# A transformer block on one core: one wide k-tile of the opening in two chunks, and the second norm's factor ahead of the last transposes

## The chip, the core and the metric

The kernel runs on one core of a Trainium2 chip. The core has a matrix engine (TensorE, PE in the profile; its weight loads are listed as PEld), a vector engine (DVE), a scalar engine (ACT), GpSimd (POOL), and a queue engine (SP) that here only issues DMAs. Each engine works through its own list of instructions in order; semaphores hold an instruction until what it needs is there. The metric is the device time of one execution in microseconds (us), the median of three runs.

## The reference, cut to what matters

A residual block on 256 tokens of width 2048, all in 32-bit floats: a norm, one input projection that gives the columns of an attention and of a convolution, an output projection with a residual, a second norm, and a gated feed-forward layer of 5632 hidden columns.

```python
xn = rms_norm(h, norm1_g)
proj = einsum('bsd,dn->bsn', xn, w_in)          # 5120 columns: q, k, v and conv
att = diff_attention(q, k, v, lam); u = conv(...)
h = h + einsum('bsm,md->bsd', concat(att, u), w_out)
hn = rms_norm(h, norm2_g)                        # the second norm
a, bu = einsum(hn, w_gate), einsum(hn, w_up)
h = h + einsum('bsf,fd->bsd', silu(a) * bu, w_down)
```

## The kernel before, in words

**Split products.** Each 32-bit product is made of three matmuls: operands are split into a high part (`hi`, a cast on ACT) and a rest (`lo`, a subtraction on DVE), and PE adds hi·hi, lo·hi and hi·lo. So each weight tile passes through four steps: SP loads it (`raw`, L320), ACT casts it (`whi`, L325), DVE subtracts (`wlo`, L334), PE multiplies (L364, L365 with `whi`, then L370 with `wlo`). One such tile with its matmuls is a *chunk*: two k-tiles (rows of 128) by 512 columns, 512 KB and 12 matmuls. There are five `raw` buffers, three `whi` and three `wlo`. Both row blocks of 128 tokens (m = 0, 1) are multiplied in each chunk.

**Order.** Python writes the instructions in one pass over the list of chunks (`run_chunks`). Ahead of each chunk's matmuls stand the load, cast and subtraction of a later chunk: one chunk ahead while the number is below `OPENING`, two ahead after that. All other work is in generators (`start`, `yield`): after the first and the second half of each chunk's matmuls each running generator is taken one step further, so a `yield` puts the next step half a chunk later on every engine's list. What a step issues stands on its engine behind what was issued before, and waits there in order.

**Opening.** The first two 512-column blocks of the input projection (`("i", 0)` and `("i", 1)`) are accumulated together, so that the first k-tiles of x are used twice while x still arrives. K-tile 0 comes in two chunks of 512 columns (256 KB each, 6 matmuls each), k-tiles 1 to 3 in one chunk each of 1024 columns (512 KB, 12 matmuls, L397, L398, L402 in `multiply_wide`), the rest as everywhere. `XLOADS` says ahead of which chunk which k-tiles of x are loaded (L484); `x_split` casts and subtracts x (`xhi` on ACT, `xlo` on DVE). All these loads stand in one queue, SP's.

**Second norm.** `out_done(n)` takes 512 finished columns of the output projection, adds them to h (DVE, L822), transposes h in two steps of two 128-column tiles (PE, `ps_h`, L832), scales and splits them (ACT L837, L839, DVE L840), takes sums of squares (ACT, L478) and sends h to DRAM (issued by POOL). After the last n = 3 the sums are reduced (DVE, L851) and `rsqrt_mean` gives the factor `rstd` on POOL (L222, L223). Then `make_forms` starts: it spreads the factor over the columns (`rep` on ACT, L976; two transposes `ps_r` on PE, L980; `rb` copied by ACT, L983), multiplies the transposed h (`hn`) by it in four steps (DVE, L988), and makes hi and lo of it (`chi`, `clo`) and seven sums with their hi and lo (`sums`, `fhi`, `flo`), which the feed-forward layer needs from its second block on. The first block of the feed-forward layer, 16 chunks of `w_gate` and `w_up`, needs none of them, and runs meanwhile on the unscaled h. In the text its chunks are counted t0 to t15; t3 is the one at whose end the new order transposes the factor.

**Pairs.** The later blocks have chunks of another kind (`wb`, `wt`, `wh`, `wlt`, `wlb`; L1041 to L1070): 21 matmuls whose operands DVE and ACT prepare from sums of weights. `hn` lies in the buffers of `wb`, so the first pair's loads wait for the last reads of `hn`.

Of the kernel before, what the change touches and what calls it, by code (L numbers as in the profile page):

```python
# [12 lines left out]
F32 = mybir.dt.float32  # L13
F32R = mybir.dt.float32r
AF = mybir.ActivationFunctionType
ALU = mybir.AluOpType
AX = mybir.AxisListType

P = 128
D = 2048  # L20
S = 256
NM = S // P
# [8 lines left out]
KD = D // P  # L31
N = 512

LINE = 128
EPS = 1e-6
# [13 lines left out]
NK = 2  # L49

WARM = 17

WIDE = 4
XLOADS = {0: range(0, 1), 2: range(1, 2), 3: range(2, 4), 5: range(4, 8), 7: range(8, 12), 9: range(12, 16)}
XSQUARES = 4

XWHOLE = 40

OPENING = 2 + WIDE - 1 + (KD - WIDE) // NK

CONV_TILES = 2

# [66 lines left out]
def tile_block(  # L129
# [6 lines left out]
    act, dve, pool, pe, sp = nc.scalar, nc.vector, nc.gpsimd, nc.tensor, nc.sync  # L136
# [8 lines left out]
    small = prestack.enter_context(tc.tile_pool(name="small", bufs=4))  # L145
# [4 lines left out]
    h = [pre.tile([P, D], F32, tag=f"h{m}", name=f"h{m}", bufs=1) for m in range(NM)]  # L150
    away = ctx.enter_context(tc.tile_pool(name="away", bufs=1, space=bass.MemoryType.DRAM))
    hd = [away.tile([P, D], F32, tag=f"hd{m}", name=f"hd{m}") for m in range(NM)]
# [65 lines left out]
    def rsqrt_mean(dst, ss, n, eps):  # L218

        k = dst.shape[-1]  # L220
        t = small.tile([P, 8], F32, tag="rsq", name="rsq")
        pool.tensor_scalar(t[:, :k], ss, 1.0 / n, eps, ALU.mult, ALU.add)  # L222
        pool.tensor_tensor(dst, t[:, :k], neghalf[:, :k], ALU.pow)  # L223
# [69 lines left out]
    def block(w, cols, ks, xs, done=None, bkey=None, first=True, last=True, spare=False, cuts=()):  # L293

        ks = list(ks)
        cols = [(cols, N)] if isinstance(cols, int) else cols
        width = sum(n for _, n in cols)
        bkey = bkey if bkey is not None else ("b", len(chunks))
        i = 0
        cuts = list(cuts)  # L300
        while i < len(ks):
            part = ks[i : i + (cuts.pop(0) if cuts else NK * N // width)]
            i += len(part)
            chunks.append(dict(w=w, ks=part, k0=part[0], nk=len(part), cols=cols, width=width, xs=xs, bkey=bkey,
                               first=part[0] == ks[0] and first, last=last and i == len(ks),
                               done=done if i == len(ks) else None, spare=spare, by_dma=False,
                               rows=slice(part[0], part[-1] + 1), load=load_chunk, round=round_chunk,
                               split=split_chunk, multiply=multiply))
# [167 lines left out]
    def square_sum(src, accum, **kw):  # L476
        junk = pre.tile([P, N], F32, tag="junk", name="junk", bufs=1)
        act.activation(junk[:, : src.shape[-1]], src, AF.Square, accum_out=accum, **kw)  # L478
# [336 lines left out]
    ss2 = [const.tile([P, 4], F32, tag=f"ss2_{m}", name=f"ss2_{m}") for m in range(NM)]  # L815
    rstd2s = const.tile([P, NM], F32, tag="rstd2", name="rstd2")
    rstd2 = [rstd2s[:, m : m + 1] for m in range(NM)]

    def out_done(n, ps):
        cs = slice(n * N, (n + 1) * N)  # L820
        for m in range(NM):
            dve.tensor_tensor(h[m][:, cs], h[m][:, cs], ps[m], ALU.add)  # L822
        if n == 2:
            held[0] -= NM
        yield
        for t in range(0, N // P, 2):
            k = n * (N // P) + t
            yield from room(1)
            pt = aux_ps.tile([P, 2, S], F32, tag="aux", name="ps_h")
            for i in range(2):  # L830
                for m in range(NM):
                    pe.transpose(pt[:, i, m * P : (m + 1) * P], h[m][:, (k + i) * P : (k + i + 1) * P], ident)  # L832
            if k % HK == 0:
                hn.append(early.tile([P, HK, S], F32, tag="wb", name="hn"))
            rows = hn[k // HK][:, k % HK : k % HK + 2, :]
            for i in range(2):
                act.activation(rows[:, i, :], pt[:, i, :], AF.Copy, scale=col("g2", k + i))  # L837
            hi, lo = lhs_two("h", k)
            act.copy(hi, rows)  # L839
            dve.tensor_tensor(lo, rows, hi.bitcast(F32), ALU.subtract)  # L840
            for i in range(2):
                hT[k + i] = (hi[:, i, :], lo[:, i, :])
            yield
        for m in range(NM):
            square_sum(h[m][:, cs], ss2[m][:, n : n + 1])
            pool.dma_start(out=hd[m][:, cs], in_=h[m][:, cs])
        if n == D // N - 1:
            yield
            ss = small.tile([P, NM], F32, tag="ssh", name="ssh")
            for m in range(NM):  # L850
                dve.tensor_reduce(ss[:, m : m + 1], ss2[m], AX.X, ALU.add)  # L851
            rsqrt_mean(rstd2s, ss, D, EPS)
            yield
            yield
            prestack.close()
            ffn["pool"] = ctx.enter_context(tc.tile_pool(name="ffn", bufs=1))
            start(make_forms())
# [114 lines left out]
    def make_forms():  # L972
        fp = ffn["pool"]
        rep = fp.tile([P, S], F32, tag="sum1", name="rep")
        for m in range(NM):
            act.activation(rep[:, m * P : (m + 1) * P], ident, AF.Identity, bias=rstd2[m], scale=0.0)  # L976
        yield
        ps = aux_ps.tile([P, N], F32, tag="aux", name="ps_r")
        for m in range(NM):
            pe.transpose(ps[:, m * P : (m + 1) * P], rep[:, m * P : (m + 1) * P], ident)  # L980
        yield
        rb = fp.tile([P, S], F32, tag="sum2", name="rb")
        act.copy(rb, ps[:, :S])  # L983
        yield
        for i in range(2):
            for k in range(0, HK, 4):
                t = hn[i][:, k : k + 4, :]
                dve.tensor_tensor(t, t, rb.unsqueeze(1).to_broadcast([P, 4, S]), ALU.mult)  # L988
                yield

        nr = HK - NS
        chi = fp.tile([P, 2 * nr, S], F32R, tag="chi", name="chi")
        clo = fp.tile([P, 2 * nr, S], F32R, tag="clo", name="clo")
        for i in range(2):
            act.copy(chi[:, i * nr : (i + 1) * nr], hn[i][:, NS:])
        yield
        for i in range(2):
            dve.tensor_tensor(clo[:, i * nr : (i + 1) * nr], hn[i][:, NS:],
                              chi[:, i * nr : (i + 1) * nr].bitcast(F32), ALU.subtract)
            yield  # L1000
        forms.update(plain={k: (chi[:, i, :], clo[:, i, :]) for i, k in enumerate(REST)})
        a11, a21 = (hn[0][:, :NS, m * P : (m + 1) * P] for m in range(NM))
        a12, a22 = (hn[1][:, :NS, m * P : (m + 1) * P] for m in range(NM))
        fhi = fp.tile([P, 7, NS, P], F32R, tag="fhi", name="fhi")
        flo = fp.tile([P, 7, NS, P], F32R, tag="flo", name="flo")
        f = fp.tile([P, 7, NS, P], F32, tag="wh", name="sums", bufs=2)
        dve.scalar_tensor_tensor(f[:, 4], a21, -1.0, a22, ALU.mult, ALU.subtract)
        dve.scalar_tensor_tensor(f[:, 5], f[:, 4], -1.0, a11, ALU.mult, ALU.subtract)
        act.copy(fhi[:, 0], a11)
        act.copy(fhi[:, 1], a12)  # L1010
        act.activation(fhi[:, 3], a22, AF.Copy, scale=-1.0)
        yield
        dve.tensor_tensor(f[:, 6], a11, a21, ALU.subtract)
        dve.tensor_tensor(f[:, 2], a12, f[:, 5], ALU.subtract)
        act.copy(fhi[:, 4:7], f[:, 4:7])
        act.copy(fhi[:, 2], f[:, 2])
        yield
        for i, a in ((0, a11), (1, a12)):
            dve.tensor_tensor(flo[:, i], a, fhi[:, i].bitcast(F32), ALU.subtract)
        yield  # L1020
        dve.scalar_tensor_tensor(flo[:, 3], a22, -1.0, fhi[:, 3].bitcast(F32), ALU.mult, ALU.subtract)
        dve.tensor_tensor(flo[:, 2], f[:, 2], fhi[:, 2].bitcast(F32), ALU.subtract)
        yield
        dve.tensor_tensor(flo[:, 4:7], f[:, 4:7], fhi[:, 4:7].bitcast(F32), ALU.subtract)
        forms.update(pair={f: (fhi[:, f], flo[:, f]) for f in range(7)})
# [246 lines left out]
    fx, fh = xT.get, hT.get  # L1272
# [2 lines left out]
    for b in range(2):  # L1275
        done += [lambda ps, key=key, b=b: qk_done(key, b, ps) for key in "kq"]
    done += [lambda ps, b=b: v_done(b, ps) for b in range(2)]
    for i in range(2):
        block(w_in, i * N, range(1), fx, bkey=("i", i), last=False, spare=i == 1)
    for k in range(1, WIDE):  # L1280
        block(w_in, [(0, 2 * N)], range(k, k + 1), fx, bkey=("i",), first=False, last=False)
        chunks[-1]["multiply"] = multiply_wide
    for i, d in enumerate(done):
# [83 lines left out]
```

## Time and profile before

| | us |
|---|---|
| median of 3 runs (lowest, highest) | 1034.31 (1033.91, 1034.35) |
| the profiled execution | 1033.71 |
| its span, first to last instruction | 1031.9 |
| PE busy | 1026.1 |
| DVE busy | 928.7 |
| ACT busy | 643.2 |
| POOL busy | 103.0 |

The span lies 1.8 us below the profiled execution's own time; this is what lies around the instructions. The execution is 0.60 us below the median of the runs. Timelines below have as columns: start and length in us, engine, line, operation, tiles written and read, shapes, count, and in brackets the idle time ahead and what ended it. A matmul's length is that of its whole passage, and matmuls overlap: what counts is the distance from one start to the next, about 0.23 us for 512 columns.

### The profile page before, as it was taken

To read this page: it belongs to the slowest core of one execution; us is meant where nothing else is said; L and a number is where in the kernel's file an instruction comes from. 1 tells how busy PE (TensorE), PEld (TensorE's weight loads), DVE (VectorE), ACT (ScalarE), POOL (GpSimd) and SP (SyncE) were. 2 spreads that over 40 slices of the span, in tenths; PEclk is the share of its full clock that TensorE was granted. 3 is DMA by queue.
4 is the path that set the end of the run, shared out by engine and by line. 5 is a ranking of instruction groups with operands and counts; after the bars stand their busy time and mean duration, and the time that the engine had idled before them with its cause. 6 is when DMAs were issued, how large, how long until landed. Compare 5 with 4: busy or idle time off the path is not lost.

```text
span 1031.9 us, 13028 instructions
## 1 busy us (share of the span) xinstructions
PE 1026.1 (99%) x4642; PEld 849.3 (82%) x4642; DVE 928.7 (90%) x1127; ACT 643.2 (62%) x785; POOL 103.0 (10%) x146
## 2 busy tenths in 40 slices
PE   9999999999999999999999999999999999999998
PEld 7888888888888888888888888888888888888887
DVE  6899999999766699999999898989999989889998
ACT  7644656665756575677666556666757556657562
POOL 0300112110000100100102111001000111010020
PEclk9999999999999999999999999999999999999999
DMA  9757555444466677987989899889798979897776
GB/s 339 245 202 253 196 184 164 153 174 162 145 212 216 187 258 226 287 257 212 259 253 261 268 248 277 259 232 266 222 266 255 284 207 289 245 270 215 227 200 173
DMA packets 116304, 238.64 MB, mean 231 GB/s; under 512 B 7824, under 2 KB 9104, under 8 KB 116240
## 3 DMA queue, kind: packets, MB, share of 16 engines
q1 hardware_dynamic: 105072, 203.58, 59.5%
q0 software_dynamic: 10880, 34.08, 17.1%
q8 instruction: 36, 0.59, 0.2%
q14 instruction: 28, 0.23, 0.1%
q10 hardware_dynamic: 288, 0.16, 0.1%
HBM read 204.24 MB, written 9.44 MB: 207 GB/s over the span
## 4 chain that ended last, share of the span: by engine, by line
PE 99%; DMA 1%; SPq 0%; ACT 0%; issue 0%; DVE 0%
PE q L1089 11%; PE q L1090 11%; PE q L1095 11%; PE acc L370 11%; PE acc L365 11%; PE acc L364 11%; PE q L1070 9%; PE q L1069 9%; PE q L1068 9%; PE ps_a L890 1%; DMA raw<-in_w_in_dram 1%; PE ps_s L711 1%; PE ps_o L781 1%; PE ps_h L832 0%; PE ps_qk L692 0%; PE acc L397 0%
## 5 line engine op out<-in xcount | busy, mean ns | idle before, releaser
L325 ACT CAST whi<-raw 128x1024 fp32r<-128x1024 f32 (+1 forms) x255 | 264.1, 1047 | 141.6 <-PE acc L365 85.8
L334 DVE TENSOR_TENSOR wlo<-raw,whi 128x1024 fp32r<-128x1024 f32 (+1 forms) x207 | 249.6, 1216 | 39.9 <-ACT whi L325 39.9
L1047 ACT CAST wh<-wt 128x2048 fp32r<-128x2048 f32 x61 | 116.8, 1915 | 111.5 <-DVE wt L1043 111.2
L1051 DVE TENSOR_TENSOR wlt<-wt,wh 128x2048 fp32r<-128x2048 f32 x61 | 139.7, 2290 | 19.8 <-ACT wh L1047 19.7
L1089 PE MATMUL q<-whi,chi 128*128 128x512 f32 x320 | 125.3, 392 | 0.0
L1090 PE MATMUL q<-whi,clo 128*128 128x512 f32 x320 | 124.7, 390 | 0.0
L364 PE MATMUL acc<-whi,xhi 128*128 128x512 f32 x308 | 122.7, 398 | 0.0
L365 PE MATMUL acc<-whi,xlo 128*128 128x512 f32 x308 | 120.5, 391 | 0.0
L1068 PE MATMUL q<-wh,fhi 128*128 128x512 f32 x280 | 109.9, 392 | 0.0
L1069 PE MATMUL q<-wh,flo 128*128 128x512 f32 x280 | 109.1, 390 | 0.0
L1050 DVE TENSOR_TENSOR wlb<-wb,wh 128x1536 fp32r<-128x1536 f32 x61 | 106.8, 1751 | 1.0 <-ACT wh L1044 1.0
L571 DVE SCALAR_TENSOR_TENSOR y<-upad,cw,y 128x256 f32<-128x256 f32 x240 | 100.9, 480 | 0.1
L329 POOL DMA_DIRECT2D wlo<-raw x48 | 41.5, 866 | 548.3 <-ACT wlo L328 318.4
L1044 ACT CAST wh<-wb 128x1536 fp32r<-128x1536 f32 x61 | 89.9, 1473 | 0.7 <-DMA wb<-in_w_down_dram 0.7
L1095 PE MATMUL q<-wlo,chi 128*128 128x512 f32 x320 | 85.6, 389 | 0.0
L370 PE MATMUL acc<-wlo,xhi 128*128 128x512 f32 x308 | 83.8, 393 | 0.0
L1041 DVE TENSOR_TENSOR wt<-wb 128x1024 f32<-128x1024 f32 x61 | 74.3, 1218 | 0.0
L1089 PE MATMUL q<-whi,ahi 128*128 128x512 f32 x182 | 71.1, 391 | 0.0
L1090 PE MATMUL q<-whi,alo 128*128 128x512 f32 x182 | 70.9, 390 | 0.0
L1095 PEld LDWEIGHTS q<-wlo,chi 128*128 128x128 f32 x320 | 60.1, 188 | 12.4
L1089 PEld LDWEIGHTS q<-whi,chi 128*128 128x128 f32 x320 | 60.1, 188 | 12.3
L1090 PEld LDWEIGHTS q<-whi,clo 128*128 128x128 f32 x320 | 60.1, 188 | 12.2
(260 smaller groups left out, 1855.2 us busy)
## 6 DMA issues: line engine op xcount, KB each, us to landing
raw<-in_w_in_dram SPq DMA_DIRECT2D x79, 512.0 KB, 4.7
raw<-in_w_gate_dram SPq DMA_DIRECT2D x48, 512.0 KB, 5.1
raw<-in_w_up_dram SPq DMA_DIRECT2D x48, 512.0 KB, 5.4
wlo<-raw POOLq DMA_DIRECT2D x48, 512.0 KB, 7.2
raw<-in_w_down_dram SPq DMA_DIRECT2D x46, 512.0 KB, 6.7
wb<-in_w_down_dram SPq DMA_DIRECT2D x42, 512.0 KB, 5.8
wb<-in_w_up_dram SPq DMA_DIRECT2D x40, 512.0 KB, 4.8
wb<-in_w_gate_dram SPq DMA_DIRECT2D x40, 512.0 KB, 5.9
```

The source lines that it names most:

```text
L325: act.copy(c["hi"], c["raw"])
L334: dve.tensor_tensor(c["lo"], c["raw"], c["hi"].bitcast(F32), ALU.subtract)
L364: pe.matmul(ps[m], xhi[:, ms], hi[:, j, :], start=c["first"] and j == 0, stop=False)
L365: pe.matmul(ps[m], xlo[:, ms], hi[:, j, :], start=False, stop=False)
L370: pe.matmul(ps[m], xhi[:, ms], lo[:, j, :], start=False, stop=c["last"] and j == nk - 1)
L1047: act.copy(c["hi"][:, :SUMMED], c["t"])
L1051: dve.tensor_tensor(lot, c["t"], c["hi"][:, :SUMMED].bitcast(F32), ALU.subtract)
L1068: pe.matmul(ps, hi, c["hi"][:, w], start=bool(first), stop=False)
L1069: pe.matmul(ps, lo, c["hi"][:, w], start=False, stop=False)
L1089: pe.matmul(ps, xs[i][0][:, ms], hi[:, i, :], start=i == 0 and bool(c["first"].get(qs[m])), stop=False)
L1090: pe.matmul(ps, xs[i][1][:, ms], hi[:, i, :], start=False, stop=False)
L1095: pe.matmul(sum_bank(c, qs[m]), xs[i][0][:, ms], lo[:, i, :], start=False, stop=i == 1 and bool(c["last"].get(qs[m])))
```

## The change

There are three edits.

1. K-tile 1 of the opening is no longer one chunk of 1024 columns but two of 512, as k-tile 0 was. There is one chunk more, so `OPENING` is 12 in place of 11 and the keys of `XLOADS` move by one. `XWHOLE`, the chunk ahead of which x is loaded once more for the residual, stays 40, so those four loads stand one chunk of work earlier on SP.
2. In `out_done(3)` the squares stand right behind the addition, and the reduction and the factor one step later, ahead of the transposes of h. The two pauses ahead of `make_forms` stay; it starts one step earlier.
3. In `make_forms` a pause is moved from behind the casts of `fhi` 4 to 6 and 2 to ahead of them.

```diff
+NARROW = 2
 WIDE = 4
-XLOADS = {0: range(0, 1), 2: range(1, 2), 3: range(2, 4), 5: range(4, 8), 7: range(8, 12), 9: range(12, 16)}
+XLOADS = {0: range(0, 1), 2: range(1, 2), 4: range(2, 4), 6: range(4, 8), 8: range(8, 12), 10: range(12, 16)}
...
-OPENING = 2 + WIDE - 1 + (KD - WIDE) // NK
+OPENING = 2 * NARROW + WIDE - NARROW + (KD - WIDE) // NK
...
+    def h_squares(n, cs):
+        for m in range(NM):
+            square_sum(h[m][:, cs], ss2[m][:, n : n + 1])
+            pool.dma_start(out=hd[m][:, cs], in_=h[m][:, cs])
...
-        yield
+        if n == D // N - 1:
+            h_squares(n, cs)
+            yield
+            ss = small.tile([P, NM], F32, tag="ssh", name="ssh")
+            for m in range(NM):
+                dve.tensor_reduce(ss[:, m : m + 1], ss2[m], AX.X, ALU.add)
+            rsqrt_mean(rstd2s, ss, D, EPS)
+        else:
+            yield
         for t in range(0, N // P, 2):
...
-        for m in range(NM):
-            square_sum(h[m][:, cs], ss2[m][:, n : n + 1])
-            pool.dma_start(out=hd[m][:, cs], in_=h[m][:, cs])
-        if n == D // N - 1:
-            yield
-            ss = small.tile([P, NM], F32, tag="ssh", name="ssh")
-            for m in range(NM):
-                dve.tensor_reduce(ss[:, m : m + 1], ss2[m], AX.X, ALU.add)
-            rsqrt_mean(rstd2s, ss, D, EPS)
+        if n < D // N - 1:
+            h_squares(n, cs)
+        else:
             yield
             yield
             prestack.close()
...
         dve.tensor_tensor(f[:, 2], a12, f[:, 5], ALU.subtract)
+        yield
         act.copy(fhi[:, 4:7], f[:, 4:7])
         act.copy(fhi[:, 2], f[:, 2])
-        yield
...
-    for i in range(2):
-        block(w_in, i * N, range(1), fx, bkey=("i", i), last=False, spare=i == 1)
-    for k in range(1, WIDE):
+    for k in range(NARROW):
+        for i in range(2):
+            block(w_in, i * N, range(k, k + 1), fx, bkey=("i", i), first=k == 0, last=False, spare=i == 1)
+    for k in range(NARROW, WIDE):
```

On ACT in the opening, the rows from the casts of k-tile 0 (`x2`) to that of k-tile 2; `xhi` is the high part of x. Before:

```order
L325 CAST whi<-raw 128x512 x2
L238 ACTIVATE xhi_140<-qT,cols 128x256
L325 CAST whi<-raw 128x1024
L238 ACTIVATE xhi_182<-qT,cols 128x256
L325 CAST whi<-raw 128x1024
```

And after the change (its lines are one higher here):

```order
L326 CAST whi<-raw 128x512 x2
L239 ACTIVATE xhi_140<-qT,cols 128x256
L326 CAST whi<-raw 128x512 x2
L239 ACTIVATE xhi_194<-qT,cols 128x256
L326 CAST whi<-raw 128x1024
```

The third row is the one that changes, from one cast to two; SP's loads, DVE's subtractions and PE's matmuls change at the same place in the same way.

On ACT from the last pieces of h to the casts of `hn`; `junk,ss` are the squares, `rep` and `rb` the factor on its way to the columns. Before:

```order
L837 ACTIVATE hn<-ps_h,cols 128x256 x2
L839 CAST hhi_3360<-hn 128x512
L478 ACTIVATE junk,ss_0_136<-h_81 128x512
L478 ACTIVATE junk,ss_1_137<-h_82 128x512
L325 CAST whi<-raw 128x1024 x2
L976 ACTIVATE rep<-ident,rstd_138 128x128 x2
L325 CAST whi<-raw 128x1024
L983 COPY rb<-ps_r 128x256
L325 CAST whi<-raw 128x1024 x3
L995 CAST chi<-hn 128x1024 x2
L325 CAST whi<-raw 128x1024
```

And after:

```order
L851 ACTIVATE hn<-ps_h,cols 128x256 x2
L853 CAST hhi_3379<-hn 128x512
L326 CAST whi<-raw 128x1024 x2
L984 ACTIVATE rep<-ident,rstd_138 128x128 x2
L326 CAST whi<-raw 128x1024
L991 COPY rb<-ps_r 128x256
L326 CAST whi<-raw 128x1024 x2
L1003 CAST chi<-hn 128x1024 x2
L326 CAST whi<-raw 128x1024 x2
```

The two squares have gone from here (they stand ahead of the first `hn<-ps_h` of n = 3), and one cast of a weight tile, that of t9, has come to stand behind the two `chi`.

On DVE from the factor's first use to the sums; `wlo` are the weight tiles' rests. Before:

```order
L334 TENSOR_TENSOR wlo<-raw,whi 128x1024 x3
L988 TENSOR_TENSOR hn<-hn,rb 128x1024 x2
L334 TENSOR_TENSOR wlo<-raw,whi 128x1024
L988 TENSOR_TENSOR hn<-hn,rb 128x1024 x2
L334 TENSOR_TENSOR wlo<-raw,whi 128x1024
L998 TENSOR_TENSOR clo<-hn,chi 128x1024
L334 TENSOR_TENSOR wlo<-raw,whi 128x1024
L998 TENSOR_TENSOR clo<-hn,chi 128x1024
L1007 SCALAR_TENSOR_TENSOR sums<-hn 128x512
```

And after:

```order
L335 TENSOR_TENSOR wlo<-raw,whi 128x1024 x3
L996 TENSOR_TENSOR hn<-hn,rb 128x1024
L335 TENSOR_TENSOR wlo<-raw,whi 128x1024
L996 TENSOR_TENSOR hn<-hn,rb 128x1024 x2
L335 TENSOR_TENSOR wlo<-raw,whi 128x1024
L996 TENSOR_TENSOR hn<-hn,rb 128x1024
L335 TENSOR_TENSOR wlo<-raw,whi 128x1024
L1006 TENSOR_TENSOR clo<-hn,chi 128x1024 x2
L335 TENSOR_TENSOR wlo<-raw,whi 128x1024
L1015 SCALAR_TENSOR_TENSOR sums<-hn 128x512
```

The work on `hn` and its forms stands half a chunk earlier among the weight tiles: the first `hn` ahead of t7's `wlo` in place of behind it. On PE the two `ps_r` transposes move from the middle of t4 to its start; POOL's list does not change.

## The prediction

> **What bounds the kernel now.** I read the page first, then PE's own waits, then the timelines around the two waits that these name, and last the DMA windows of the opening.
>
> ```profile
> span 1031.9 us, 13028 instructions
> PE 1026.1 (99%) x4642; PEld 849.3 (82%) x4642; DVE 928.7 (90%) x1127; ACT 643.2 (62%) x785; POOL 103.0 (10%) x146
> PE 99%; DMA 1%; SPq 0%; ACT 0%; issue 0%; DVE 0%
> ```
>
> The third line is the chain that ended last: it is PE nearly from end to end. The change takes no matmul away and adds none (k-tile 1 is 12 matmuls either way), so it can only move the time in which PE stands still. Who made PE wait, in total, times, longest:
>
> ```profile
> PE acc L397 <- ACT whi L325: 0.6, 1, 0.6
> PEld acc L370 <- DVE wlo L334: 0.5, 1, 0.5
> PEld q L1070 <- DVE wlt L1051: 0.7, 2, 0.5
> ```
>
> These are three places: k-tile 1 of the opening, the end of the first feed-forward block, and the first pair behind it. What each costs PE is read from starts.
>
> ```profile
> 8.00 0.62 PE L370 MATMUL acc<-wlo,xhi 128*128 128x512 f32 x2
> 9.23 0.50 PE L397 MATMUL acc<-whi,xhi 128*128 128x512 f32 x1 [0.60 <-ACT whi L325]
> 9.57 0.40 PE L398 MATMUL acc<-whi,xlo 128*128 128x512 f32 x1
> 12.09 0.39 PE L397 MATMUL acc<-whi,xhi 128*128 128x512 f32 x1
> ...
> 372.78 0.39 PE L364 MATMUL acc<-whi,hhi 128*128 128x512 f32 x1
> 375.50 0.39 PE L364 MATMUL acc<-whi,hhi 128*128 128x512 f32 x1
> 378.55 0.39 PE L364 MATMUL acc<-whi,hhi 128*128 128x512 f32 x1
> ...
> 386.95 0.39 PE L1069 MATMUL q<-wh,flo 128*128 128x512 f32 x1
> 387.71 0.40 PE L1068 MATMUL q<-wh,fhi 128*128 128x512 f32 x1
> ```
>
> A chunk takes 2.72 (372.78 to 375.50), so a start-to-start step is 2.72/12 = 0.227. Opening: two steps behind 8.00 is 8.45, the start was 9.23 and the next step took 0.34, so PE lost 0.78 + 0.11 = 0.89. Chunk t13 took 3.05, a loss of 0.33. Two steps at the pair took 0.76 in place of 0.45, a loss of 0.31. Together 1.5 us, 0.15% of the time: this is all that the change can win at the places it touches.
>
> **Edit 1, k-tile 1 in two chunks.** One subtraction and ACT's rows of the opening:
>
> ```profile
> 4.76 0.69 DVE L334 TENSOR_TENSOR wlo<-raw,whi 128x512 fp32r<-128x512 f32 x1 [0.56 <-ACT whi L325]
> ...
> 4.11 0.62 ACT L325 CAST whi<-raw 128x512 fp32r<-128x512 f32 x1 [0.43 <-DMA raw<-in_w_in_dram]
> 5.35 0.62 ACT L325 CAST whi<-raw 128x512 fp32r<-128x512 f32 x1 [0.62 <-DMA raw<-in_w_in_dram]
> 6.87 0.51 ACT L238 ACTIVATE xhi<-qT,cols 128x256 fp32r<-128x256 f32 x1 [0.90 <-DMA qT<-in_xt_dram]
> 8.13 1.05 ACT L325 CAST whi<-raw 128x1024 fp32r<-128x1024 f32 x1 [0.75 <-DMA raw<-in_w_in_dram]
> 10.76 1.05 ACT L325 CAST whi<-raw 128x1024 fp32r<-128x1024 f32 x1 [0.86 <-DMA raw<-in_w_in_dram]
> ```
>
> ACT's rows bracket a wait for a DMA each: the loads land one behind the other and ACT takes each as it lands. K-tile 1's 512 KB took from 6.87 to 8.13. Its first half, loaded alone, lands about half way, near 7.6; the cast of 512 columns takes 0.62 in place of 1.05, to 8.2; PE can go on at 8.45 without a gap. The second half lands at 8.13 or a little later, is cast by 8.8, and PE needs it six steps on, at 9.8. So the wait at 9.23 goes. Both casts together take 0.19 more on ACT, both subtractions about 0.15 more on DVE (0.69 each, first row, against 1.23 for 1024 columns, below), all beside PE work.
>
> What is late next is k-tile 2. Its cast began at 10.76 because its data came then, and PE started on it at 12.09. By the distances of k-tile 1 (cast 8.13, first matmul 9.23, and the slow step of 0.11) PE can be at full step on k-tile 2 at 10.76 + 1.10 + 0.11 = 11.97. PE would be free for it at 8.45 + 12 × 0.227 = 11.17 and wait 0.8 there. So of 0.89 only 12.09 − 11.97 = 0.12 remains, if k-tile 2's data is as early as before. It stands in the same queue behind the same bytes, so the question is whether two loads of 256 KB pass as fast as one of 512 KB. Shorter rows do pass more slowly:
>
> ```profile
> 10.00:11.00 1.00, 1.00 (x6) 0.80 (x5) 0.83 (x2) 0.24 (x1) 0.00 (x0) 1.00 1.05 430
> 23.00:24.00 1.00, 1.00 (x6) 0.84 (x5) 1.00 (x3) 0.55 (x1) 0.00 (x0) 1.00 1.08 367
> ```
>
> The last two columns are the busy share of the DMA engines and GB/s. In the first window wide loads move (rows of 4 KB, 430), in the second those of two k-tiles by 512 (rows of 2 KB, 367), with the engines full in both. 0.524 MB takes 1.22 us at the one and 1.43 at the other, so +0.2 for k-tile 2. The bounds: 0 if the split costs nothing, and the pace of k-tile 0's two loads, 5.35 − 4.11 = 1.24 for 256 KB, so 2.48 in place of 1.26, or +1.2. I take +0.2, since it is a pace under full engines, which these are from 8 us on, while at 4 to 5 us the queue was still filling. The opening then gives 0.12 − 0.2 = −0.08, that is 0.1 us lost, between 0.12 won and 1.1 lost; below that, won up to 0.89 if k-tile 2 also comes earlier for a reason that no row shows.
>
> The Trainium skill (DMA: Bandwidth & Descriptors, Rules for kernel authors and Anatomy of one DMA) speaks against the split: for bandwidth it wants 1 MiB or more in a DMA, and it fits about 2.0 us of fixed cost to each on GpSimd's path. If that cost fell into the queue for each load, k-tile 2 would come 2.0 us later, an estimate, and the kernel would lose about 1.2 us in all (1035.5). This trace agrees with a cost for size, not with 2.0 us in line: k-tile 0's two loads came 1.24 us apart.
>
> One DMA more is issued by SP (0.46 us for each of the two behind 3.53), and with five `raw` buffers k-tile 3's load now waits for k-tile 0's first buffer, at 5.48 in place of about 4.0:
>
> ```profile
> 3.53 0.91 SPq L320 DMA_DIRECT2D raw<-in_w_in_dram x2
> 5.48 1.62 SPq L320 DMA_DIRECT2D raw<-in_w_in_dram x2
> ```
>
> That costs nothing: at 5.48 the queue still holds all up to k-tile 2, which came at 10.76. The four loads of x that move one chunk earlier cost nothing either, since behind the opening no row has ACT waiting for `in_w_in`.
>
> **Edits 2 and 3, the factor earlier.** Why DVE was late at 377 and 387:
>
> ```profile
> 340.34 1.28 DVE L822 TENSOR_TENSOR h<-h,acc 128x512 f32<-128x512 f32 x2
> 349.58 0.21 DVE L851 TENSOR_REDUCE ssh<-ss 128x1 f32<-128x4 f32 x2
> 353.48 2.45 DVE L334 TENSOR_TENSOR wlo<-raw,whi 128x1024 fp32r<-128x1024 f32 x2 [2.55 <-ACT whi L325]
> 355.84 2.35 DVE L988 TENSOR_TENSOR hn<-hn,rb 128x1024 f32<-128x1024 f32 x2
> 369.13 0.68 DVE L1014 TENSOR_TENSOR sums<-hn,sums 128x512 f32<-128x512 f32 x1
> 372.23 1.23 DVE L334 TENSOR_TENSOR wlo<-raw,whi 128x1024 fp32r<-128x1024 f32 x1 [1.21 <-ACT whi L325]
> 374.57 1.75 DVE L1024 TENSOR_TENSOR flo<-sums,fhi 128x1536 fp32r<-128x1536 f32 x1
> 376.24 3.49 DVE L334 TENSOR_TENSOR wlo<-raw,whi 128x1024 fp32r<-128x1024 f32 x3
> 379.65 1.22 DVE L1041 TENSOR_TENSOR wt<-wb 128x1024 f32<-128x1024 f32 x1
> 385.04 2.28 DVE L1051 TENSOR_TENSOR wlt<-wt,wh 128x2048 fp32r<-128x2048 f32 x1
> ...
> 346.74 0.63 ACT L478 ACTIVATE junk<-h 128x512 f32<-128x512 f32 x1
> 351.81 0.70 ACT L976 ACTIVATE rep<-ident,rstd 128x128 f32<-128x128 f32 x2 [2.46 <-POOL rstd L223]
> 361.63 1.05 ACT L995 CAST chi<-hn 128x1024 fp32r<-128x1024 f32 x1 [1.15 <-DVE hn L988]
> 378.49 1.48 ACT L1044 CAST wh<-wb 128x1536 fp32r<-128x1536 f32 x1
> ...
> 349.89 1.09 POOL L222 TENSOR_SCALAR rsq<-ssh 128x2 f32<-128x2 f32 x1 [7.44 <-DVE ssh L851]
> ```
>
> t13's `wlo` ran from 376.24 and PE stood for it until 377.51; behind it DVE runs without a gap to `wlt`, for which PE stood at 387. DVE idled before: 2.55 because t6's cast stood on ACT behind `rep`, which waited for the factor, and 1.21 because t12's cast stood behind the casts of `fhi`, which waited for `sums`.
>
> In the new order the squares follow the addition to h, which ends at 341.6: 0.63 and a read of the sum behind it, 0.75 each, to 342.5, then reduction and 1.9 us of POOL (349.89 to `rep` at 351.81), so the factor is there at about 344.7 and `rep` finds it. ACT's two squares push `hn<-ps_h` back by 0.25 and are caught up by 347.3, where they stood before; h's last tiles are needed by PE only from t6 on (356). `rep` now goes at 348.4, the transposes at 350.75, `rb` is there at 351.4. From there I walk DVE's list with the durations above: t6's `wlo` 351.0 (its `whi` buffer is free when PE has passed half of t3), first `hn` 352.1, t7 353.95 (paced by PE), two `hn` to 357.35, t8 to 358.5, the fourth `hn` to 359.65. Now comes a new wait: t9's cast stands behind the second `chi`, which waits for that `hn`, so it ends at 361.6 and DVE idles 2.0. Then, without a gap: t9, two `clo`, t10, four `sums` to 368.75 (the old end was 369.13 + 0.6 = 369.7), t11, four `flo`, t12, the long `flo`, and t13 from 375.2. All `fhi` are cast by 370.2, so the 1.21 goes. DVE is 1.04 earlier at t13 (375.2 against 376.24) and ready at 376.35; PE needs it at 377.3. `wt` starts at 378.6, where ACT reads the same `wb` already before (its cast of it began at 378.49 without a wait), and `wlt` is ready at 386.2; PE needs it at 387.18 − 0.33 = 386.85. Both waits go: 0.33 + 0.31 = 0.64. `wlo` of t9 to t12 all keep 1 us or more to their use. Bounds: 0 if DVE is not earlier at all, 0.64 from about 0.3 earlier on, since there is no more PE idle here. The moved transposes cost the same two slots on PE.
>
> **Sum.** 0.64 won − 0.08 lost = 0.56 won. Against the profiled execution, 1033.71 − 0.56 = 1033.15; this execution lies 0.60 below the median, so against the median 1034.31 − 0.56 = 1033.75, say 1033.7.
>
> **The rivals.**
> - *The factor's haste is eaten by t9.* If ACT's wait behind `chi` is 1 us longer than the 2.0 I worked out, t13 is late as before: nothing won at 377 and 387, and 1034.31 + 0.08 = 1034.4. For it: the 2.0 is new and in the chain. Against: 0.95 us of room at t13. Here the change doesn't do what it could.
> - *The slow side: two loads at k-tile 0's pace.* K-tile 2 lands 1.2 later, PE waits about 2.0 ahead of it, the opening loses 1.1: 1034.31 + 1.1 − 0.64 = 1034.8. It decides against the change once k-tile 2 comes more than 0.64 + 0.12 = 0.76 later. For it: 1.24 per 256 KB is measured in this very stage. Against: a full queue and 430 GB/s as k-tile 2 arrives. The Trainium skill's rule above is this rival with a larger price.
> - *The opening's gap really closes.* If k-tile 2 comes 0.8 earlier, all of 0.89 + 0.64 is won: 1032.8. For it: DMA is slow before 8 us and a change of row length may shift that; against: it stands behind the same bytes.
>
> **How the numbers follow.** Forecast 0.62, t9 0.13, slow side 0.12, gap closed 0.11, none of these 0.02. The likeliest is 1033.7. The range takes in the ends at 1032.8 and 1034.8, with 0.1 for the spread of runs above: 1032.8 to 1034.9. About 0.2% (2.07 us) is what a measurement of this kernel can tell from no change, and no case reaches it from either side: within 0.2% has 0.91. The rest is for what no row shows, mostly a gain or loss in DMA timing in the long later part: faster 0.05, slower 0.04.
>
> **What would show it.** Right: no PE wait on `wlo` near 377 and `wlt` near 387; `rep` without a wait for POOL; DVE idle about 2 us ahead of t9's `wlo`; PE's first matmul of k-tile 1 at about 8.5 and a wait of about 0.8 to 1.0 ahead of k-tile 2's first. Wrong: that wait gone or near 2 us; a new row in PE's waits; a median more than 1 us from 1033.7.

## The result and the profile after

| | before | after |
|---|---|---|
| median of 21 runs each, us | 1034.11 | 1032.55 |
| lowest, highest | 1033.50, 1036.39 | 1031.88, 1033.13 |
| the profiled execution, us | 1033.71 | 1032.55 |
| its span, us | 1031.9 | 1030.8 |

The ratio is 0.9983, with a 95% interval of 0.9977 to 0.9989: 1.56 us or 0.15% less. The change is within 0.2%, as forecast, but nearly three times the 0.56 of the sum, and the time lies below the range, which ended at 1032.8. Of the 1.20 us between the forecast 1033.75 and the measured 1032.55, 1.00 is the change and 0.20 the starting point: the median of the kernel before was 1034.31 over three runs and is 1034.11 over 21.

The page of the kernel after, its span, busy times and chain:

```profile
span 1030.8 us, 13034 instructions
PE 1025.7 (100%) x4642; PEld 849.4 (82%) x4642; DVE 929.2 (90%) x1128; ACT 643.4 (62%) x786; POOL 102.7 (10%) x146
PE 100%; POOL 0%; DVE 0%; issue 0%; POOLq 0%
```

DMA, ACT and SP's queue, which stood in the chain before, are gone from it. Who makes PE's weight loads wait in the kernel after (in total, times, longest), without the three rows for the warm-up, the transposes of h and the attention (1.4, 0.9 and 0.8 us), which are the same before and after:

```profile
PEld q L1103 <- DMA wlo<-raw: 0.3, 1, 0.3
PEld q L1078 <- DVE wlt L1059: 0.2, 1, 0.2
```

The rows for `wlo` and for `whi` of k-tile 1 are gone; the wait for `wlt` is down from 0.7 to 0.2. The row with DMA is new. It costs 0.16 us at 880 and is not there in the second profile of the kernel after. The timeline of the opening in the kernel after, ACT's rows and then PE's:

```profile
5.75 0.51 ACT L239 ACTIVATE xhi<-qT,cols 128x256 fp32r<-128x256 f32 x1
6.65 1.37 ACT L326 CAST whi<-raw 128x512 fp32r<-128x512 f32 x2 [0.40 <-DMA raw<-in_w_in_dram]
10.29 1.05 ACT L326 CAST whi<-raw 128x1024 fp32r<-128x1024 f32 x1 [0.81 <-DMA raw<-in_w_in_dram]
...
6.75 0.81 PE L371 MATMUL acc<-wlo,xhi 128*128 128x512 f32 x2
7.40 0.40 PE L365 MATMUL acc<-whi,xhi 128*128 128x512 f32 x1
8.79 0.39 PE L365 MATMUL acc<-whi,xhi 128*128 128x512 f32 x1
11.07 0.62 PE L371 MATMUL acc<-wlo,xhi 128*128 128x512 f32 x2
11.53 0.39 PE L398 MATMUL acc<-whi,xhi 128*128 128x512 f32 x1
```

K-tile 1 starts at 8.79 (9.23 before) and k-tile 2 at 11.53 (12.09 before), neither with a gap ahead of it: 11.07 to 11.53 is two steps of 0.23. PE came to k-tile 1 at 8.79 and not at the forecast 8.45 by its own pace: its first steps took 0.43 or more, until 7.2 in this profile and until 6.3 in that of the kernel before. K-tile 2's cast began at 10.29, not at 10.76 as before. The timeline of the later part of the kernel after, DVE's rows, then ACT's, then PE's:

```profile
361.39 1.22 DVE L335 TENSOR_TENSOR wlo<-raw,whi 128x1024 fp32r<-128x1024 f32 x1 [2.06 <-ACT whi L326]
374.82 3.49 DVE L335 TENSOR_TENSOR wlo<-raw,whi 128x1024 fp32r<-128x1024 f32 x3
383.62 2.29 DVE L1059 TENSOR_TENSOR wlt<-wt,wh 128x2048 fp32r<-128x2048 f32 x1
...
347.74 0.69 ACT L984 ACTIVATE rep<-ident,rstd 128x128 f32<-128x128 f32 x2
359.36 1.05 ACT L1003 CAST chi<-hn 128x1024 fp32r<-128x1024 f32 x1 [2.16 <-DVE hn L996]
...
376.76 1.07 PE L371 MATMUL acc<-wlo,hhi 128*128 128x512 f32 x4
377.66 0.39 PE L365 MATMUL acc<-whi,hhi 128*128 128x512 f32 x1
386.05 0.39 PE L1077 MATMUL q<-wh,flo 128*128 128x512 f32 x1
386.28 0.39 PE L1078 MATMUL q<-wlt,fhi 128*128 128x512 f32 x1
386.50 0.39 PE L1076 MATMUL q<-wh,fhi 128*128 128x512 f32 x1
```

`rep` finds the factor without a wait. T13's `wlo` starts at 374.82 in place of 376.24. PE passes t13's four matmuls with `wlo` in 0.90 and the first pair in steps of 0.23: both gaps are closed. New is DVE's idle time of 2.06 ahead of t9's `wlo`.

Where the 1.1 us between the two spans comes from is read by setting each matmul of one trace against the same one of the other. The kernel after is 0.55 ahead from k-tile 2 on and still 0.56 at 370, 0.90 behind t13, 1.25 behind the first pair, and 1.10 at the end (the wait for a DMA above costs the last 0.16). So the opening gave 0.55 and the later part 0.7, less that wait. That the medians differ by 1.56 and not by 1.1 is the first hint that the profile of before was not a typical execution.

### The profile page after: what moved, and what is told of

Same layout as the page of the kernel before. It is cut to its first block, busy times and chain, and to the rows that moved or that the text cites. A ratio compares the mean times of both kernels' runs of the same rounds, so it can differ in the third digit from the quotient of the medians.

```text
span 1030.8 us, 13034 instructions
## 1 busy us (share of the span) xinstructions
PE 1025.7 (100%) x4642; PEld 849.4 (82%) x4642; DVE 929.2 (90%) x1128; ACT 643.4 (62%) x786; POOL 102.7 (10%) x146
## 4 chain that ended last, share of the span: by engine, by line
PE 100%; POOL 0%; DVE 0%; issue 0%; POOLq 0%
PE acc L365 11%; PE acc L366 11%; PE acc L371 11%; PE q L1097 11%; PE q L1103 11%; PE q L1098 11%; PE q L1078 9%; PE q L1077 9%; PE q L1076 9%; PE ps_a L898 1%; PE ps_s L712 1%; PE ps_o L782 1%; PE ps_warm L164 0%; PE ps_h L846 0%; PE ps_qk L693 0%; PE ps_at L802 0%
```

## The experiments

"Won" and "lost" are against the median of the kernel before, run on the same chip: 1033.93 in the first group (33 runs), 1033.96 in the second (33), 1034.02 in the third (27). Each kernel ran 11 times, `factor_only` 5 times.

### First group: one part at a time

Both kernels once more, without an edit:

> The kernel before, unchanged, profiled once more: how far does the opening vary from one execution to the next? Theory L (luck of the DMA): x's k-tile 1 lands anywhere between 5.7 and 6.9 us and k-tile 2's weights between 10.2 and 10.9, whatever the kernel, and the changed kernel's opening was a lucky one. Theory S (the split makes it so): x's k-tile 1 is cast near 6.9 again, k-tile 1's weights near 8.1, k-tile 2's near 10.8, PE waits 0.6 ahead of k-tile 1. Time: no change, within 0.2 us of 1034.1.

> The changed kernel unchanged, profiled once more. Theory S: no wait of PE in the opening, k-tile 2's weights cast before 10.5. Theory L: k-tile 2's weights may come as late as 10.9, PE waiting up to 0.8 ahead of them. Time 1032.5 by both, 1.5 below before.

Measured: 1034.01 (ratio 0.9998, 0.9989 to 1.0007) and 1032.38 (0.9983, 0.9975 to 0.9992). The second profile of the kernel before shows another opening than the first; its timeline, ACT and PE:

```profile
7.06 0.51 ACT L238 ACTIVATE xhi<-qT,cols 128x256 fp32r<-128x256 f32 x1 [0.70 <-DMA qT<-in_xt_dram]
8.41 1.04 ACT L325 CAST whi<-raw 128x1024 fp32r<-128x1024 f32 x1 [0.84 <-DMA raw<-in_w_in_dram]
10.41 1.05 ACT L325 CAST whi<-raw 128x1024 fp32r<-128x1024 f32 x1 [0.55 <-DMA raw<-in_w_in_dram]
...
7.66 0.40 PE L370 MATMUL acc<-wlo,xhi 128*128 128x512 f32 x1
9.51 0.50 PE L397 MATMUL acc<-whi,xhi 128*128 128x512 f32 x1 [1.44 <-ACT whi L325]
12.36 0.39 PE L397 MATMUL acc<-whi,xhi 128*128 128x512 f32 x1
```

PE stood 1.44 us here, not 0.60: its last matmul of k-tile 0 started at 7.66, against 8.00 and a step (8.23) in the first profile, and k-tile 1's weights came 0.28 later (8.41 against 8.13). K-tile 2's cast, on the other hand, began at 10.41 in place of 10.76. So neither theory fits this profile whole: x's k-tile 1 was late, as by theory S, and k-tile 2's weights moved, as by theory L.

Edit 1 alone:

```diff
+NARROW = 2
-XLOADS = {0: range(0, 1), 2: range(1, 2), 3: range(2, 4), 5: range(4, 8), 7: range(8, 12), 9: range(12, 16)}
+XLOADS = {0: range(0, 1), 2: range(1, 2), 4: range(2, 4), 6: range(4, 8), 8: range(8, 12), 10: range(12, 16)}
...
+    for k in range(NARROW):
+        for i in range(2):
+            block(w_in, i * N, range(k, k + 1), fx, bkey=("i", i), first=k == 0, last=False, spare=i == 1)
+    for k in range(NARROW, WIDE):
```

> Edit 1 alone (k-tile 1 in two chunks). By the prediction's sum: 0.1 us lost, 1034.2. By theory S: what the two other edits leave of the measured 1.56, so 0.9 to 1.0 won, 1033.1, and k-tile 2's weights are cast before 10.5 again. By theory L: a few tenths either way, and its profile can show k-tile 2 as late as 10.8 with PE waiting for it.

Measured: 1032.98, ratio 0.9990 (0.9981 to 0.9999), 0.95 won. The opening is that of the kernel after, on the timeline of ACT and PE:

```profile
6.92 0.62 ACT L326 CAST whi<-raw 128x512 fp32r<-128x512 f32 x1 [0.20 <-DMA raw<-in_w_in_dram]
7.89 0.62 ACT L326 CAST whi<-raw 128x512 fp32r<-128x512 f32 x1 [0.36 <-DMA raw<-in_w_in_dram]
10.21 1.05 ACT L326 CAST whi<-raw 128x1024 fp32r<-128x1024 f32 x1 [0.82 <-DMA raw<-in_w_in_dram]
...
8.89 0.39 PE L365 MATMUL acc<-whi,xhi 128*128 128x512 f32 x1
11.61 0.39 PE L398 MATMUL acc<-whi,xhi 128*128 128x512 f32 x1
```

The waits for t13's `wlo` (0.5) and for `wlt` (0.6) are still there. So the opening's part is edit 1's alone.

Edits 2 and 3 alone, that is the diff of `out_done` and `make_forms` with the old opening:

```diff
...
+        if n == D // N - 1:
+            h_squares(n, cs)
+            yield
...
+        yield
         act.copy(fhi[:, 4:7], f[:, 4:7])
         act.copy(fhi[:, 2], f[:, 2])
-        yield
```

> Edits 2 and 3 alone (factor earlier, pause moved). By the prediction's sum: 0.64 won, 1033.5, with no wait of PE on wlo near 377 or wlt near 387. If the later part won more than the profile of before shows (a rival for the missing 0.4 us), 1.0 or more. If the waits come back elsewhere, below 0.3.

Measured: 1033.41, ratio 0.9996 (0.9987 to 1.0005), 0.52 won. Set against the second profile of the kernel before, its matmuls are 0.14 behind just ahead of t13 and 0.55 ahead after the first pair: 0.7. The interval of the medians holds 1; it is this comparison that shows the gain. DVE's and ACT's rows on the timeline:

```profile
362.34 1.23 DVE L334 TENSOR_TENSOR wlo<-raw,whi 128x1024 fp32r<-128x1024 f32 x1 [2.06 <-ACT whi L325]
...
368.93 1.49 ACT L1023 CAST fhi<-sums 128x1536 fp32r<-128x1536 f32 x1 [2.02 <-DVE sums L1020]
370.84 2.94 ACT L325 CAST whi<-raw 128x1024 fp32r<-128x1024 f32 x3
```

The new idle time ahead of t9 is the same 2.06 as in the kernel after, so it comes from these two edits. The parts add up: 0.95 + 0.52 = 1.47, against 1.55 for both in this group.

A sharper comparison than that of the medians takes all the profiles of this document, those of the two groups below too. From the time of each profiled execution, take the start of PE on k-tile 2 (12.09 in 1033.71 for the kernel before, 11.53 in 1032.55 for the kernel after): what is left is all that lies behind the opening. It is 1021.56 to 1021.67 in the seven profiles with the old second norm and 1020.91 to 1021.05 in the six with edits 2 and 3; the kernel with edit 2 alone is left out. So the later part is 0.66 shorter with edits 2 and 3 (means 1021.63 and 1020.97), and nearly all else by which executions differ lies ahead of PE's start on k-tile 2. The medians 1034.11 and 1032.55 then stand for a start at 12.48 and at 11.58: 0.90 for edit 1.

### Second group: what of edit 1 wins

K-tile 1 in halves does two things at once: two smaller loads, and cast, subtraction and matmuls in halves. Each alone, on the kernel before. Two loads of 512 columns, with one cast and one round of matmuls as before:

```diff
-        block(w_in, [(0, 2 * N)], range(k, k + 1), fx, bkey=("i",), first=False, last=False)
+        block(w_in, [(0, N), (N, N)] if k == 1 else [(0, 2 * N)], range(k, k + 1), fx, bkey=("i",), first=False, last=False)
```

> The kernel before, with k-tile 1's 1024 columns loaded by two DMAs of 512 columns into one buffer, but cast, subtracted and multiplied as one. In four profiles so far x's k-tile 1 was cast at 6.9 to 7.0 us and k-tile 1's weights at 8.1 to 8.5 where they come in one load, and at 5.8 to 6.2 and 6.7 (first half) where they come in two. Theory D (the rows of 4 KB are what makes both late): x near 6.0, the whole of k-tile 1 landed by 7.5 to 7.9, PE on it near 8.7, 0.8 us won, 1033.1. Theory C (the gain is that PE needs only half a tile to go on; the landing is as before): x near 7.0, weights near 8.4, nothing won, 1033.9.

One load, with casts, subtractions and matmuls of 512 columns each:

```diff
+    def round_halves(c):
+        c["hi"] = c["view"](wp.tile([P, NK * N], F32R, tag="whi", name="whi", bufs=HL_BUFS))
+        for i in range(2):
+            cs = slice(i * N, (i + 1) * N)
+            act.copy(c["hi"][:, :, cs], c["raw"][:, :, cs])
...
+        if k == 1:
+            chunks[-1].update(round=round_halves, split=split_halves, multiply=multiply_halves)
```

> The kernel before, with k-tile 1 still one load, but cast, subtracted and multiplied in halves of 512 columns. Theory C: PE goes on 0.4 us after the landing is cast by half, the whole gain of edit 1, about 0.9. Theory D: landing near 8.4 as before, PE on k-tile 1 at about 9.1 in place of 9.5, 0.4 us won, 1033.5, and not more.

Two loads by partitions, 64 rows of 1024 columns each, so that rows stay 4 KB long:

```diff
...
+        for r in (slice(0, P // 2), slice(P // 2, P)):
+            sp.dma_start(out=c["raw"][r], in_=rows[r, c["rows"], : 2 * N])
...
```

> As the kernel with two loads and one cast, but each load has 64 partitions by the whole 1024 columns, so the two DMAs are as many bytes each while their rows stay 4 KB. If the length of the rows makes x's k-tile 1 late: x near 7.0 and weights near 8.4 again, nothing won, 1033.9. If the size of one DMA does: x near 6.0, as with two loads of 512 columns, 0.8 won.

K-tile 2 in halves as well, on the kernel after:

```diff
-NARROW = 2
+NARROW = 3
-XLOADS = {0: range(0, 1), 2: range(1, 2), 4: range(2, 4), 6: range(4, 8), 8: range(8, 12), 10: range(12, 16)}
+XLOADS = {0: range(0, 1), 2: range(1, 2), 4: range(2, 4), 7: range(4, 8), 9: range(8, 12), 11: range(12, 16)}
```

> The changed kernel with k-tile 2 in two chunks as well. Its profile shows no wait of PE in the opening any more, or 0.03 us, so by theory C nothing is left to win: 1032.4. By theory D k-tile 2's rows of 4 KB no longer hold up the load of x's k-tiles 2 and 3 ahead of it (cast near 8.9), and k-tile 2 comes earlier than 10.2; still PE can use it only from 11.5 on: 1032.4 too, 0.1 won at most.

| | median | ratio (95%) | won | PE's wait ahead of k-tile 1 |
|---|---|---|---|---|
| two loads | 1033.50 | 0.9996 (0.9987 to 1.0005) | 0.46 | 0.2 |
| two casts | 1033.60 | 0.9997 (0.9988 to 1.0005) | 0.36 | 0.3 |
| half rows | 1034.36 | 1.0005 (0.9996 to 1.0014) | -0.40 | 1.3 |
| k-tile 2 too | 1032.31 | 0.9983 (0.9974 to 0.9992) | 1.65 | none |

The intervals of the first three hold 1, so each single gain is no more than likely; the traces say more than the times. The two theories gave one of the single parts a gain of 0.8 or 0.9 and the other 0.4 or nothing; the medians lie between. K-tile 2 in halves won 1.65, against 1.55 for the kernel after in the first group: no difference that these runs can tell. On the timelines, two loads:

```profile
8.07 1.05 ACT L325 CAST whi<-raw 128x1024 fp32r<-128x1024 f32 x1 [1.07 <-DMA raw<-in_w_in_dram]
10.21 1.05 ACT L325 CAST whi<-raw 128x1024 fp32r<-128x1024 f32 x1 [0.68 <-DMA raw<-in_w_in_dram]
...
9.18 0.50 PE L397 MATMUL acc<-whi,xhi 128*128 128x512 f32 x1 [0.17 <-ACT whi L325]
```

Two casts:

```profile
8.20 1.14 ACT L410 CAST whi<-raw 128x512 fp32r<-128x512 f32 x2 [1.10 <-DMA raw<-in_w_in_dram]
...
8.87 0.49 PE L424 MATMUL acc<-whi,xhi 128*128 128x512 f32 x1 [0.27 <-ACT whi L410]
```

And half rows:

```profile
5.39 0.50 ACT L238 ACTIVATE xhi<-qT,cols 128x256 fp32r<-128x256 f32 x1
8.73 1.04 ACT L332 CAST whi<-raw 128x1024 fp32r<-128x1024 f32 x1 [2.84 <-DMA raw<-in_w_in_dram]
10.72 1.05 ACT L332 CAST whi<-raw 128x1024 fp32r<-128x1024 f32 x1 [0.54 <-DMA raw<-in_w_in_dram]
```

With one cast the first matmul starts 1.11 behind the start of the cast (8.07 to 9.18), with two 0.67 (8.20 to 8.87): halving the work gives 0.44. Halving the loads gives about as much in the medians; in its profile the weights came at 8.07, at the early end of what whole loads had (8.04 to 8.74), so earlier data is the likely way. Neither alone is edit 1; the two sum to 0.82, near its 0.95, but each interval reaches 0.9 us to either side, so the sum proves little.

With load and cast both halved, PE can multiply the first half while the second is still on its way. In the kernel after and with edit 1 alone PE came too late for this: it started at 8.79 and 8.89, when both halves were cast. It shows in the kernel with k-tile 2 in halves too, where PE came to k-tile 1 early, at 7.98, and the second half's cast began only at 8.91:

```profile
8.91 0.62 ACT L326 CAST whi<-raw 128x512 fp32r<-128x512 f32 x1 [1.29 <-DMA raw<-in_w_in_dram]
...
7.98 0.39 PE L365 MATMUL acc<-whi,xhi 128*128 128x512 f32 x1
```

Half rows speak against the number of loads as the cause. With 4 KB rows two loads brought the weights at 8.73, no earlier than one load did, and k-tile 2 at 10.72, although x came early (5.39). But this is one profile, and these loads also fill 64 partitions each and not 128.

### Third group: the pause, and who sets the opening's pace

Edit 2 without edits 1 and 3, so with the pause behind the casts of `fhi` as before:

```diff
...
+        if n == D // N - 1:
+            h_squares(n, cs)
+            yield
...
         act.copy(fhi[:, 4:7], f[:, 4:7])
         act.copy(fhi[:, 2], f[:, 2])
         yield
```

> Edits 1 and 3 taken out: the factor early, the pause in its old place. On ACT the casts of fhi 4 to 6 and 2 then stand ahead of the two sil and of t11's cast, and wait for the sums. By the walk along DVE's list, with the times of the profile that has edits 2 and 3 alone: the casts at 368.9, sil behind them, t11's cast at 372.0 in place of 365.9, its wlo ready at 374.1 where PE needs it at 372.3, so PE stands about 1.8 there and 0.9 more at t12: 2.2 us slower than before, 1036.1. Rival: the pause is of no weight, PE has room: 1033.4, as with edits 2 and 3.

Measured: 1037.48, ratio 1.0037 (1.0024 to 1.0049), 3.46 lost. The timeline, ACT, DVE and PE:

```profile
369.15 1.49 ACT L1022 CAST fhi<-sums 128x1536 fp32r<-128x1536 f32 x1 [4.11 <-DVE sums L1020]
372.20 2.93 ACT L325 CAST whi<-raw 128x1024 fp32r<-128x1024 f32 x3
...
373.27 1.23 DVE L334 TENSOR_TENSOR wlo<-raw,whi 128x1024 fp32r<-128x1024 f32 x1 [3.56 <-ACT whi L325]
...
369.75 1.07 PE L370 MATMUL acc<-wlo,hhi 128*128 128x512 f32 x4
373.30 0.50 PE L364 MATMUL acc<-whi,hhi 128*128 128x512 f32 x1 [2.48 <-ACT whi L325]
374.33 0.57 PE L364 MATMUL acc<-whi,hhi 128*128 128x512 f32 x1
375.13 0.63 PE L364 MATMUL acc<-whi,hhi 128*128 128x512 f32 x1
375.98 1.91 PE L370 MATMUL acc<-wlo,hhi 128*128 128x512 f32 x4
377.69 0.45 PE L364 MATMUL acc<-whi,hhi 128*128 128x512 f32 x1
```

With the earlier start one weight cast less stands ahead of the casts of `fhi`. ACT stands 4.11 us at the head of its list for `sums`, the weight cast that PE needs stands behind it, and PE stands 2.48 us for `whi` at 373.30. With the pause moved (the edits 2 and 3 above) ACT's wait there is 2.02, since two activations (`sil`) and a weight cast fill the rest, and PE does not wait. So edit 3 is what makes edit 2 pay. The window view of the same kernel, of which the columns behind the busy times are the granted clock, DMA's share and GB/s:

```profile
373.00:374.50 1.50, 1.21 (x5) 1.02 (x6) 1.23 (x2) 1.50 (x3) 0.00 (x0) 0.96 0.00 0
374.50:378.00 3.50, 3.50 (x10) 2.68 (x10) 3.50 (x6) 1.68 (x2) 0.00 (x0) 0.53 0.63 200
378.00:380.00 2.00, 2.00 (x10) 1.67 (x9) 2.00 (x3) 0.23 (x1) 0.00 (x0) 1.00 1.06 410
```

Behind the stand the clock was granted at 0.53 and the steps are 0.43 in place of 0.23: the eight steps from 374.33 to 377.69 took 3.36 in place of 1.82, so the wait cost 1.5 us more than itself. The loss of 2.2 us expected ahead of the run had the waits and not this.

Three kernels have another number of warm-up matmuls ahead of the opening, which moves the time at which PE is ready: two more in the kernel before, two more in the kernel after, and two fewer in the one with k-tile 2 in halves. The first two:

```diff
-WARM = 17
+WARM = 19
```

> The kernel before with 19 warm-up transposes in place of 17, so PE's first matmul starts 0.41 later, at 5.3. If the wide kernel's opening ends with the landing of k-tile 1, wherever PE stands: no loss, 1033.9 to 1034.1, k-tiles 4 and 5 begun at 17.5 to 18.0 as in the other profiles. If PE's own pace sets it: 0.4 lost, 1034.4.

> The changed kernel with 19 warm-up transposes. Its profiles show PE without a wait in the opening and k-tile 2's cast done just as PE gets there, so PE's pace sets it: 0.3 to 0.4 lost, 1032.8. If the landing of k-tile 2 set it: nothing lost, 1032.4.

And the third, on the kernel after (with `XLOADS` as for k-tile 2 in halves):

```diff
-WARM = 17
+WARM = 15
...
-NARROW = 2
+NARROW = 3
```

> Edits 1 to 3, k-tile 2 in two chunks as well, and 15 warm-up transposes. The first matmul's operands are ready at 4.6 and it starts at 4.9 behind the warm-ups, so it can start 0.3 earlier; with k-tile 2 in halves no landing is in the way: 0.2 to 0.3 won over the changed kernel, 1032.1. If fewer warm-ups only make PE's slow stretch longer, nothing is won: 1032.4 or more.

Measured: the kernel before 1033.89 (ratio 1.0000, 0.9991 to 1.0009), nothing lost; the kernel after 1032.69 (0.9987, 0.9978 to 0.9996), 1.33 won against 1.55 in the first group, which ran on another chip; the intervals overlap. PE's first matmul starts 0.43 later there (5.32 against 4.89), and the chunk of k-tiles 4 and 5 at 17.28, against 16.99 and 17.17 in the two profiles of the kernel after. So before, the landing of k-tile 1 set the opening; after, the profiles have PE's own pace set it in part, and the times cannot tell. The last kernel had 1031.93 (0.9981, 0.9972 to 0.9990), the lowest median of all, 2.09 won; its interval overlaps that of the kernel after, so that it beats the latter is likely and not shown.

## Why the prediction was right or wrong

**The bound: right.** PE bounds the kernel, the work on PE stayed (4642 matmuls), and only its standing still went. Yet the cap of 1.5 us "at the places it touches" was exceeded by the medians (1.56), if only just: it was read from one execution.

**Edits 2 and 3: right in mechanism and size.** 0.64 was forecast; the profiles show 0.66 to 0.7 and the medians 0.52, with an interval that holds 1. The steps came as worked out: `rep` without a wait, the new idle time of 2.0 ahead of t9 measured 2.06, t13's `wlo` forecast at 375.2 and, with the 0.51 us that the opening had won by then taken off, due at 374.7, measured 374.82. The rival by which t9 eats the gain did not happen: its point was 1 us more than 2.0.

**Edit 1: wrong.** The step that failed is the term 0.12 − 0.2 = −0.08: k-tile 2 was to come 0.2 later and so to leave nothing of the opening's 0.89. Measured: 0.95 won by the medians of edit 1 alone, 0.90 by the comparison over all profiles. Two things are in the difference of about 1.0.

- *The size of the old wait.* The prediction took the profiled execution's opening (0.60 of wait, PE on k-tile 2 at 12.09, of which 0.12 could be won) for that of all, and then added the 0.60 by which that execution lay below the median as a constant. It lay below because its opening was a good one: 12.09 is 0.39 ahead of the 12.48 that the median stands for, and what lies behind it took as long as in the others. In the second profile of the kernel before the same reckoning gives 12.36 - (10.41 + 1.10 + 0.11) = 0.74 to be won in place of 0.12. In the other three profiles with one load and whole casts it gives 0.52 (edits 2 and 3 alone), 0.75 (edit 2 alone) and 0.48 (19 warm-ups): the 0.12 was the smallest of five. This is 0.4 to 0.6 of the difference. The waits ahead of k-tile 1 in these three were 1.74, 1.58 and 0.59.
- *K-tile 2's data came earlier, not later.* Its cast began between 10.31 and 10.78 in the five profiles with one load and whole casts for k-tile 1, between 10.02 and 10.49 in the five with two loads of 512 columns and k-tile 2 whole. (The ranges overlap, and with one load and halved casts it was 10.20, so that two loads are the cause is likely and not shown.) With 10.29 + 1.10 the data allowed PE to start at 11.39, before PE was through with k-tile 1. In the second profile of the kernel after it was 10.49, and PE began on k-tile 2 at 11.59, just with the data: this load is next in line. The +0.2 came from the pace of full engines (430 and 367 GB/s). K-tile 1's halves moved earlier: from 5 to 8 us the profile before, with the wide load, had 274 to 293 GB/s in each window of 1 us, so the two paces of the sum were not those of this place.

The third rival, "the opening's gap really closes", with 0.11, is what happened to PE, but not by its condition. K-tile 2 came 0.47 earlier in the profile of the kernel after (10.29 against 10.76), not 0.8, and that was enough only because PE, with its slow first steps, came to k-tile 2 at 11.53 and not at 11.17. The rival's 1.53 taken from the median of 21 runs would have given 1032.58; that the measured 1032.55 lies so near is in part luck, since its 0.89 was read from that one good opening.

Of its other words on edit 1, the two casts and subtractions cost nothing, and neither did the later load of k-tile 3. The first half of k-tile 1, said to land near 7.6, was cast from 6.65, as x had come earlier too. The wait of 0.8 to 1.0 ahead of k-tile 2 that was to show it right was not there; this was named as a sign of the contrary.

The rule of the Trainium skill (DMA: Bandwidth & Descriptors, Rules for kernel authors) that wants 1 MiB or more in a DMA is one for bandwidth, and these runs do not bear it out at this place: with loads of 256 KB in place of 512 KB, and the work halved with them, the kernel was 0.95 us faster; with the loads alone it was 0.46, which the interval does not tell from nothing. PE waited here for the first columns of one tile.

**Left open.** Why x's k-tile 1, which stands ahead of k-tile 1's weights in the queue in both kernels, is cast at 6.2 to 7.1 with one wide load behind it and at 5.75 to 6.2 in the kernels with edit 1. Two loads with one cast had 6.50, half rows 5.39, so it is neither row length nor the number of loads alone. That x came earlier was not enough for the gain: with half rows it came earliest and PE waited 1.31. Also open is what ends PE's slow first steps: those of 0.43 lasted until 7.2 in all four profiles whose opening is that of the kernel after, while in six of the 14 profiles there was none, and the granted clock reads 1.00 over them (4.90 to 7.40 us in the kernel after).

## What to carry to other kernels

A wait that ends with a DMA early in the kernel differs between executions by as much as its size: bound it by two or three profiles, and when the profiled execution lies below the median, ask which wait made it so, before the difference is added as a constant. At a start where the engine that bounds waits for data, halve the load and the work on it together; each alone won about half here, and neither clear of noise. A step moved earlier on an in-order engine can put a wait at the head of that engine's list: move what it holds up, too, as the pause does here (0.52 won with it, 3.46 lost without).

## What was not expected of the hardware

A stand of PE of 2.48 us was followed by 3.4 us at a granted clock of about half (0.53), which cost 1.5 us more. The Trainium skill (TensorE: Matmul & The Clock Gate, Part 1) tells of an activity window of about 3.4 us that runs on its own and by which the clock is set; the length of the slow stretch agrees. The same page (Why this matters for your kernels) advises against idle gaps of PE of more than about 3 us; here a shorter one was enough. The stands of 1.3 to 1.7 us at k-tile 1 show no such stretch behind them.
